# Turning attention weights for former keys in 32x32 squares on VectorE and through device memory, in a two-layer hybrid encoder kernel

## The chip, the core and the metric

The kernel runs on one core of a Trainium2 chip. The metric is the time of one execution in microseconds (us) of device time; lower is better. The kernel before was run three times: 2492.28, 2494.07 and 2495.88 us. The core's engines are TensorE (PE; PEld is its loading of stationary operands), VectorE (DVE), ScalarE (ACT), GpSimd (POOL) and SyncE (SP), which here issues every DMA.

## What is computed

Two layers over a sequence of 2048 frames of width 1024, batch 1. Each layer normalises and modulates its input, maps it by one combined projection, runs two groups of heads on the result, and maps their outputs back by one projection onto the residual. The change touches the second group, four heads of differential attention, shortened here:

```
def diff_branch(q, k, v, z, qn_g, kn_g, lam, lam_init, g_out):
    q = rms_norm(q.reshape(B, S, 4, 2, 64), qn_g) * 64 ** -0.5
    k = rms_norm(k.reshape(B, S, 4, 2, 64), kn_g)
    ...
    s = einsum('bqhmd,bkhmd->bhmqk', qi, k)      # two score maps m per head
    p = softmax(where(key_chunk <= q_chunk, s, -inf), axis=-1)   # chunks of 64 frames
    attn = p[:, :, 0] - lam * p[:, :, 1]
    o = einsum('bhqk,bkhe->bqhe', attn, v)       # v is 128 wide
    return rms_norm(o, g_out) * (1 - lam_init) * silu(z)
```

The other group is a gated linear attention with a recurrent state per chunk. All arrays are float32.

## The kernel before

**Units.** The sequence is cut into four units of 512 frames, u = 0 to 3, and each layer goes through them in order. A unit has dense work (nine items of 512 columns: four attention heads, two groups for the convolved inputs, the gate, two halves of the output projection), the gated linear part, and the four attention heads. In the dense work every operand is split into a high and a low part, so one product is three matmuls of 128x512; an item is 8 contraction steps x 4 banks x 3 matmuls. The program calls the banks `acc`, the split weights `w`, and the split input `hhi` and `hlo`. The weights are split once per layer, kept in device memory (`wd`), and loaded again by each later unit as tiles of 512 KB, one per contraction step; pool `p_w` holds four.

**Attention.** `attn_gen(l, u, hd)` does one head of one unit. Keys and values of former units lie in device memory (`KD`, `VD`) and are loaded as `Kj` and `Vj`; those of the unit itself are `Kt` and `Vt`. The head's 512 queries are taken in four row blocks of 128, qt = 0 to 3. `scores(qt, m)` multiplies queries by keys into PSUM (`sc`); VectorE moves the negated scores to a row `s` of 128 x 2048 in SBUF with a running minimum, and ScalarE takes the exponent of the row. When both maps of a row block are there, VectorE combines them in place into the attention weights `at`, by `scalar_tensor_tensor` over pieces of 512 (`s<-s,r` in the profile); the second row, `b`, is free then.

`pv(qt)` multiplies the weights by the values. That product contracts over keys, so keys must lie along the partitions, while a row of `at` has queries there. Each 128x128 square is turned by a transpose on TensorE against the identity (`tp<-ident,s`); ScalarE copies four squares at a time from PSUM to an SBUF tile (`aT<-tp`), and each square is the stationary operand of one float32 matmul with 128 columns of values (`po<-Vj,aT`, `po<-Vt,aT`), which the profile shows as two weight loads and two matmuls. Row block qt of unit u has 4u + qt + 1 squares, 4u of them for former units: 1088 squares in the whole kernel.

**Pools.** `p_s` has four score rows, so the scores of two row blocks are ahead; `p_at` holds three tiles of turned weights. `p_q` has five slots of 4 KB per partition, used by the input blocks `xt`, by three tiles of the gated linear part, and by the split queries `qh` and `ql` of each head. `ps_t` holds four PSUM banks, shared by `sc`, `tp` and `po`.

**Order of the work.** The code is written as streams (dense, attention, query/key, gated linear, preparation), merged by the TensorE time that each step declares. `record` only stores each operation. Then `Program.order`, a list scheduler that knows the pools, a cost for each operation (`cost`) and delays between engines (`LAT`), and models the DMA queue as one server, sets the order on each engine; `best_order` repeats that with small changes and keeps the best by its own reckoning. What comes out is a fixed order for each engine: on the chip each engine runs its own list in order, and waits where an operand is late. SP's list is one too: a DMA that has to wait holds up all DMAs listed behind it. Since all operations are issued at one place, line 370, the profile is read by tile names rather than lines.

Of the kernel before, what the change touches and what calls it, by code (L numbers as in the profile page):

```python
# [12 lines left out]
F32 = mybir.dt.float32  # L13
# [9 lines left out]
P = 128  # L23
D = 1024
KT = D // P
UT = 512
# [94 lines left out]
class Program:  # L121
# [53 lines left out]
    @staticmethod  # L175
    def cost(e, method, args, kw, out):
        n = math.prod(out.shape[1:])
        if e == "S":
            return math.prod(out.shape) * 4 / 360.0
        if e == "T":  # L180
            if method == "transpose":
                return 110
            rate = {F32R: 2.4, BF16: 2.4, F32: 0.6}[args[2].dt]
            if rate == 0.6 and args[1].shape[1] < P:
                return 54 if args[1].shape[0] == CH else 60
            return max(n * 0.444, 112 * args[1].shape[1] / P) if rate == 2.4 else max(n / rate, 216) + 6
# [187 lines left out]
def trunk_kernel(ctx, tc, x, c, w_ada, b_ada, norm_g, w_in, conv_w, w_gk, b_gk, gla_norm_g,  # L374
# [232 lines left out]
    def done(*ev):  # L607
        events[ev] = clock[0]
# [224 lines left out]
    def gla_gen(l, u):  # L833
# [146 lines left out]
        for hd in range(4):  # L980
# [3 lines left out]

    KD = [[dram.tile([P, 2, UT], F32, name=f"kd{u}_{h}") for h in range(4)] for u in range(NU - 1)]
    VD = [[dram.tile([P, TT, P], F32, name=f"vd{u}_{h}") for h in range(4)] for u in range(NU - 1)]
    WD = [[[dram.tile([P, 2, 512], F32, name=f"wd{l}_{i}_{k}") for k in range(KT)] for i in range(9)]
          for l in range(L)]
    XD = [dram.tile([UT, D], F32, name=f"xd{u}") for u in range(NU)]
# [27 lines left out]
    def qk_gen(l, u, hd):  # L1017
        y = layers[l]
        key = l * NU + u
        yield need("hev", key, hd, lag=6.0)  # L1020
        qk, Vt, sz = HD.pop((key, hd))
        qh = p_q.tile([P, 2, UT], F32R, tag="q", name="qh")
        ql = p_q.tile([P, 2, UT], F32R, tag="q", name="ql")
        Kt = p_kv.tile([P, 2, UT], F32R, tag="K", name="Kt")
        for g in range(2):
            ps = tp()
            for t in range(TT):
                T.transpose(ps[:, t * P:(t + 1) * P], qk[t][:, g * P:(g + 1) * P], ident)
# [16 lines left out]
        done("qkT", key, hd)  # L1045

    def attn_gen(l, u, hd):
# [12 lines left out]
        Ks.append(Kt)  # L1060
# [3 lines left out]
        def scores(qt, m):  # L1064
# [23 lines left out]
            if m == 1:  # L1088
# [9 lines left out]
                q_t[qt] = (at, r, clock[0] + 0.6 + 0.00083 * nk + 0.4 + 0.5 + 0.8)  # L1098

        def pv(qt):  # L1100
            at, r, t0 = q_t.pop(qt)
            nk = u * UT + (qt + 1) * P
            qs = slice(qt * P, qt * P + P)
            nb = nk // P
            o_ = po()[:, 0:P]
            if t0 > clock[0]:
                yield pe(0, t0 - clock[0])
            prev = None

            def mmv(g0, w, aT):  # L1110
                for i in range(w):
                    T.matmul(o_, aT[:, i * P:(i + 1) * P], Vs[g0 // 4][:, i, :],
                             start=(g0 + i == 0), stop=(g0 + i == nb - 1))

            for g0 in range(0, nb, 4):
                w = min(4, nb - g0)
# [3 lines left out]
                aT = p_at.tile([P, 512], F32, tag="aT", name="aT")  # L1120
                A.copy(aT[:, 0:w * P], ps[:, 0:w * P])
                yield pe(0.11 * w, 0 if prev else 0.9)
                if prev:
                    mmv(*prev)
                    yield pe(0.22 * prev[1], 0.2)
                prev = (g0, w, aT)
            if nb > 4:
                yield pe(0, 0.7)
            mmv(*prev)
            yield pe(0.22 * prev[1])  # L1130
# [6 lines left out]
            V.scalar_tensor_tensor(sz[:, qt, :], o_, wq, sz[:, qt, :], op0=ALU.mult, op1=ALU.mult)  # L1137

        seq = [(qt, m) for qt in range(TT) for m in range(2)]
        order = [("s", 0), ("s", 1), ("s", 2), ("s", 3)]  # L1140
        for qt in range(TT):
            order.append(("c", qt))
            for x_ in (2 * qt + 4, 2 * qt + 5):
                if x_ < 2 * TT:
                    order.append(("s", x_))
        for k_, i in order:
# [196 lines left out]
```

## Time and profile before

| | |
|---|---|
| median of 3 runs | 2494.07 us |
| lowest and highest | 2492.28, 2495.88 us |
| span of the profiled execution | 2491.1 us, clock 0.999 |
| TensorE busy | 2454.7 us |
| VectorE busy | 1690.3 us |
| ScalarE busy | 1369.9 us |
| moved by DMA | 473.99 MB, 190 GB/s in the mean |

For the profiled execution the page gives its span alone, 2491.1 us, from the first to the last instruction; no time of its own stands beside that. The median of the three timed runs is 3.0 us above the span. Busy time of TensorE is no measure of its spare time, because matmuls overlap in the pipeline and their ends are modelled. More is told by the chain of work that ended last, in which each step is followed back to what released it: there, a stretch that belongs to TensorE alone is one that gets shorter when TensorE has less to do. First layer: unit 1 is worked on from about 300 us, unit 2 from about 600, unit 3 from about 900 to 1130. Second layer: units 1, 2 and 3 from about 1560, 1870 and 2180 us; the last instruction is at 2491.

### The profile page before, as it was taken

The numbers are of one execution on the slowest core, as the hardware profiler recorded it, in microseconds if no ns is written. First come the engines' busy times: TensorE is split into PE (matmuls) and PEld (weight loads), VectorE is DVE, ScalarE is ACT, GpSimd is POOL, SyncE is SP. The second block draws the span as 40 slices with busy tenths as digits, with TensorE's granted clock in tenths as the row PEclk, the third lists the DMA queues.
The fourth block names the chain that finished last, engine by engine and source line by source line (L and its number), as shares of the span: only waits on it lengthen the run. The fifth ranks groups of instructions, "written<-read, shape, count | busy, mean of one in ns | idle before, by whom it ended". The sixth has DMA issues, their size and how long they took to land.

```text
span 2491.1 us, 40404 instructions
## 1 busy us (share of the span) xinstructions
PE 2454.7 (99%) x13923; PEld 2027.2 (81%) x13923; DVE 1690.3 (68%) x4993; ACT 1369.9 (55%) x3080; POOL 133.0 (5%) x424
## 2 busy tenths in 40 slices
PE   8999999999999999999999999999999999999998
PEld 5787788888888878888788777888788888888887
DVE  4879777772768727678764894667636777276873
ACT  5757545572556724556763583556625567155652
POOL 0001000000000000000000010000000000000000
PEclk9999999999999999999999999999999999999999
DMA  8778866457453563435367877455464444633343
GB/s 264 265 238 294 309 236 213 149 193 240 146 175 117 195 211 121 157 127 173 112 206 258 283 254 266 164 179 180 165 227 157 150 155 155 217 132 127 124 148 127
DMA packets 204684, 473.99 MB, mean 190 GB/s; under 512 B 20736, under 2 KB 82368, under 8 KB 204480
## 3 DMA queue, kind: packets, MB, share of 16 engines
q1 hardware_dynamic: 204480, 471.41, 55.6%
q8 instruction: 111, 1.82, 0.3%
q14 instruction: 93, 0.76, 0.1%
HBM read 360.19 MB, written 111.15 MB: 189 GB/s over the span
## 4 chain that ended last, share of the span: by engine, by line
PE 83%; DVE 8%; DMA 4%; ACT 2%; issue 2%; POOL 0%; SPq 0%; POOLq 0%; DVEq 0%; ACTq 0%
PE acc L370 54%; PE sc L370 11%; PE po L370 10%; PE tp L370 8%; DVE s L370 3%; DMA wr<-in_w_ada_dram 2%; DVE t L370 1%; DMA wd<-w 1%; DVE am L370 1%; DVE w L370 1%; DMA xt<-in_x_dram 1%; ACT s L370 1%; DMA raw<-in_w_in_dram 0%; ACT qh L370 0%; SPq L370 0%
## 5 line engine op out<-in xcount | busy, mean ns | idle before, releaser
L370 PE MATMUL acc<-w,hhi 128*128 128x512 f32 x2560 | 832.5, 402 | 0.6 <-DVE rt L370 0.3
L370 PEld LDWEIGHTS acc<-w,hhi 128*128 128x128 f32 x2560 | 463.1, 189 | 85.1 <-issue 3.0
L370 PE MATMUL acc<-w,hlo 128*128 128x512 f32 x1280 | 505.6, 395 | 0.0
L370 ACT ACTIVATE s<-s,mx 128x512 f32<-128x512 f32 (+15 forms) x256 | 308.2, 1204 | 238.1 <-DVE s L370 236.5
L370 PE MATMUL acc<-hhi,w 128*128 128x512 f32 x1024 | 363.4, 401 | 0.0
L370 PE MATMUL acc<-w,oh 128*128 128x512 f32 x1024 | 332.4, 397 | 1.0 <-ACT oh L370 0.8
L370 DVE TENSOR_SCALAR_CACHE_REDUCE s<-sc,mx 64x64 f32<-64x64 f32 (+5 forms) x640 | 308.6, 485 | 36.2 <-PE sc L370 15.2
L370 PEld LDWEIGHTS acc<-w,hlo 128*128 128x128 f32 x1280 | 240.8, 188 | 49.4 <-DVE hlo L370 0.4
L370 PEld LDWEIGHTS acc<-w,oh 128*128 128x128 f32 x1024 | 189.5, 188 | 41.5 <-DVE t L370 2.1
L370 PEld LDWEIGHTS acc<-hhi,w 128*128 128x128 f32 x1024 | 191.7, 188 | 35.8 <-DVE z L370 0.3
L370 DVE TENSOR_SCALAR_CACHE_REDUCE s<-sc 128x512 f32<-128x512 f32 (+4 forms) x256 | 158.3, 622 | 75.4 <-PE sc L370 72.0
L370 PE MATMUL po<-Vj,aT 128*128 128x128 f32 x1536 | 204.2, 276 | 2.5 <-ACT aT L370 2.2
L370 PE MATMUL acc<-w,ol 128*128 128x512 f32 x512 | 202.8, 397 | 0.0
L370 PE MATMUL acc<-hlo,w 128*128 128x512 f32 x512 | 201.0, 393 | 0.0
L370 PEld LDWEIGHTS po<-Vj,aT 128*128 128x128 f32 x1536 | 190.8, 192 | 11.4 <-ACT aT L370 5.8
L370 DVE SCALAR_TENSOR_TENSOR s<-s,r 128x512 f32<-128x512 f32 (+2 forms) x320 | 197.8, 667 | 2.7
L370 ACT COPY aT<-tp 128x512 f32<-128x512 f32 (+2 forms) x320 | 163.3, 521 | 61.3 <-PE tp L370 59.6
L370 ACT COPY rw<-acc 128x256 f32<-128x256 f32 x128 | 48.0, 375 | 252.7 <-PE acc L370 252.4
L370 PE MATMUL tp<-ident,s 128*128 128x128 f32 x1088 | 174.3, 275 | 6.9 <-DVE s L370 6.2
L370 PEld LDWEIGHTS tp<-ident,s 128*128 128x128 f32 x1088 | 132.8, 141 | 42.5 <-issue 8.9
L370 PE MATMUL sc<-Kj,qh 128*128 128x512 f32 x384 | 158.5, 413 | 1.6 <-DVE s L370 0.9
L370 ACT CAST w<-raw 128x512 fp32r<-128x512 f32 x152 | 93.5, 627 | 107.4 <-PE acc L370 89.5
(184 smaller groups left out, 3708.5 us busy)
## 6 DMA issues: line engine op xcount, KB each, us to landing
w<-wd SPq DMA_DIRECT2D x424, 512.0 KB, 4.1
wd<-w SPq DMA_DIRECT2D x144, 512.0 KB, 4.5
raw<-in_w_in_dram SPq DMA_DIRECT2D x120, 256.0 KB, 4.7
Kj<-kd SPq DMA_DIRECT2D x48, 512.0 KB, 4.6
wr<-in_w_ada_dram SPq DMA_DIRECT2D x128, 128.0 KB, 3.7
kd<-Kt SPq DMA_DIRECT2D x24, 512.0 KB, 2.6
Vj<-vd SPq DMA_DIRECT2D x48, 256.0 KB, 3.8
wr<-in_w_ada_dram SPq DMA_DIRECT2D x8, 1024.0 KB, 9.6
```

The costliest lines, as they stand in the source:

```text
L370: getattr(self.engines[e], method)(*[real(a) for a in args], **{k: real(v) for k, v in kw.items()})
```

## The change

For former units, in units 1 and 2 with all four heads and in unit 3 with heads 0 to 2 (`turned`), the squares are no longer turned on TensorE. After the combination, VectorE turns the former part of the row in 32x32 squares, from `at` into `b`, in two instructions that each take every other group of 128 columns and write every other element. One DMA writes `b` to device memory (`AD`) in pieces of 1 KB; another reads it back into `at` with the 32-row groups put in place, in pieces of 64 elements (256 bytes). The keys then lie on the partitions in an order of their own, so the values of former units are kept a second time in that order (`VP`, copied from `VD` within device memory once per head and unit) and read from there. `pv` takes the stationary operands straight from `at`, every second element. The squares of the unit itself (1 to 4 per row block) are still turned on TensorE, first of all, and copied by ScalarE into `b`. Where nothing is turned (unit 0; head 3 of unit 3) the old path remains, with `b` in place of the tile `aT`.

`p_s` grows to five rows, `p_at` is gone, `p_q` shrinks to four slots. Turned heads begin with five score rows instead of four. The planner reckons DMAs whose last dimension is 64 at 256 bytes per ns instead of 360, and the stream waits 7 us of TensorE time longer before `pv`.

```diff
-            return math.prod(out.shape) * 4 / 360.0
+            return math.prod(out.shape) * 4 / (256.0 if out.shape[-1] == 64 else 360.0)
...
-    p_s = pool("p_s", 4)
-    p_at = pool("p_at", 3)
+    p_s = pool("p_s", 5)
...
-    p_q = pool("p_q", 5)
+    p_q = pool("p_q", 4)
...
+            SY.dma_start(VP[u][hd].rearrange("(j b) t e -> j b (t e)", b=4),
+                         VD[u][hd].rearrange("(b j) t e -> j b (t e)", b=4))
...
+        turned = u > 0 and (u < NU - 1 or hd < 3)
...
-            SY.dma_start(b, VD[j][hd])
+            SY.dma_start(b, (VP if turned else VD)[j][hd])
...
+                if turned:
+                    turn_blocks(at, b, AD[u][TT * (hd % 2) + qt])
...
+        def turn_blocks(at, b, dr):
+
+            n = u * UT
+            src = at[:, 0:n].rearrange("p (g k a i) -> p g k a i", k=2, a=4, i=32)
+            dst = b[:, 0:n].rearrange("p (g a i k) -> p g k a i", a=4, k=2, i=32)
+            for k in range(2):
+                V.transpose(dst[:, :, k], src[:, :, k])
+            SY.dma_start(dr.rearrange("g p b n -> p g (b n)"), b[:, 0:n].rearrange("p (g n) -> p g n", n=256))
+            SY.dma_start(at[:, 0:n].rearrange("p (h n) -> p h n", n=64),
+                         dr.rearrange("g (a j) b n -> (j b) (g a) n", a=4))
...
+            if turned:
+                pairs = at[:, 0:u * UT].rearrange("p (g m k) -> p g k m", k=2, m=P)
+                flip(4 * u, qt + 1)
+                yield pe(0.11 * (qt + 1), 0.9)
+                mmv(4 * u, qt + 1, flat, True, False)
+                yield pe(0.22 * (qt + 1), AFTER)
+                for j in range(u):
+                    mmv(4 * j, 4, lambda k: pairs[:, k // 2, k % 2, :], False, j == u - 1)
+                    yield pe(0.88)
...
-        order = [("s", 0), ("s", 1), ("s", 2), ("s", 3)]
+        ahead = 5 if turned else 4
+        order = [("s", x_) for x_ in range(ahead)]
```

How the order changes is seen best in unit 3 of the second layer. On TensorE, before, around the last row block of head 0 (`tp<-ident,s` turns squares of weights, `po` multiplies by values, `acc` is dense work, `tp<-ident,rw` turns queries and keys of a later head):

```order
L370 MATMUL tp<-ident,s 128x128 x4
L370 MATMUL po<-Vj,aT 128x128 x4
L370 MATMUL acc<-w,hhi 128x512 x2
L370 MATMUL acc<-w,hlo 128x512
L370 MATMUL tp<-ident,rw 128x128 x4
L370 MATMUL tp<-ident,s 128x128 x4
L370 MATMUL po<-Vj,aT 128x128 x4
L370 MATMUL acc<-w,hhi 128x512 x2
L370 MATMUL acc<-w,hlo 128x512
```

On the same engine and at the same place, in the changed kernel:

```order
L370 MATMUL tp<-ident,s 128x128 x4
L370 MATMUL acc<-w,hhi 128x512 x2
L370 MATMUL acc<-w,hlo 128x512
L370 MATMUL acc<-w,hhi 128x512 x2
L370 MATMUL acc<-w,hlo 128x512
L370 MATMUL po<-Vt,s 128x128 x4
L370 MATMUL tp<-ident,z 128x128 x2
L370 MATMUL po<-Vj,s 128x128 x12
```

The transposes of former keys are gone. Only the unit's own four squares are turned, and the twelve products with former values stand in one run.

On SP, before, in the same unit, the weight tiles (`w<-wd`) of items 2 and 5, then those of item 3 and the next head's keys:

```order
L370 DMA w<-wd_5_4_14997 128x1024
L370 DMA w<-wd_5_5_15003 128x1024
L370 DMA w<-wd_5_6_15017 128x1024
L370 DMA w<-wd_5_7_15027 128x1024
L370 DMA w<-wd_3_0_15308 128x1024
L370 DMA w<-wd_3_1_15325 128x1024
L370 DMA Kj<-kd_2_2307 128x1024
```

On SP in the changed kernel, at the same place (`ad<-s` writes a turned row block, `s<-ad` reads it back):

```order
L370 DMA w<-wd_5_4_14550 128x1024
L370 DMA w<-wd_5_5_14556 128x1024
L370 DMA ad_5_11289<-s 128x6x256
L370 DMA s<-ad_5_11289 128x24x64
L370 DMA w<-wd_5_6_14570 128x1024
L370 DMA w<-wd_5_7_14580 128x1024
L370 DMA Kj<-kd_2_2308 128x1024
L370 DMA Kj<-kd_2_5130 128x1024
L370 DMA ad_6_11471<-s 128x6x256
```

A write and its reading back now stand between the weight loads, here without anything between the two, so that the loads behind them are issued only when the write has landed. Of the 88 pairs in the list, 12 stand like this and the other 76 have one to five other DMAs between write and read.

More of the change, by code (lines that the diff above doesn't have):

```diff
@@ L986, in trunk_kernel @@
     VD = [[dram.tile([P, TT, P], F32, name=f"vd{u}_{h}") for h in range(4)] for u in range(NU - 1)]
+    VP = [[dram.tile([P, TT, P], F32, name=f"vp{u}_{h}") for h in range(4)] for u in range(NU - 1)]
+    AD = [[dram.tile([2 * u, P, 4, 64], F32, name=f"ad{u}_{t}") for t in range(2 * TT)] if u else None
+          for u in range(NU)]
     WD = [[[dram.tile([P, 2, 512], F32, name=f"wd{l}_{i}_{k}") for k in range(KT)] for i in range(9)]
@@ L1043, in qk_gen @@
             SY.dma_start(VD[u][hd], Vt)
+            SY.dma_start(VP[u][hd].rearrange("(j b) t e -> j b (t e)", b=4),
+                         VD[u][hd].rearrange("(b j) t e -> j b (t e)", b=4))
         HD[key, hd, "q"] = (qh, ql, Kt, Vt, sz)
         done("qkT", key, hd)
+    WAIT, AFTER = 7.0, 0.0
     def attn_gen(l, u, hd):
@@ L1097, in scores @@
                                            op0=ALU.mult, op1=ALU.add)
-                q_t[qt] = (at, r, clock[0] + 0.6 + 0.00083 * nk + 0.4 + 0.5 + 0.8)
+                if turned:
+                    turn_blocks(at, b, AD[u][TT * (hd % 2) + qt])
+                q_t[qt] = (at, b, r, clock[0] + 0.6 + 0.00083 * nk + 0.4 + 0.5 + 0.8 + (WAIT if turned else 0))
+        def turn_blocks(at, b, dr):
[7 more added lines that the diff above has]
+                         dr.rearrange("g (a j) b n -> (j b) (g a) n", a=4))
         def pv(qt):
-            at, r, t0 = q_t.pop(qt)
-            nk = u * UT + (qt + 1) * P
+            at, b, r, t0 = q_t.pop(qt)
             qs = slice(qt * P, qt * P + P)
-            nb = nk // P
+            nb = 4 * u + qt + 1
             o_ = po()[:, 0:P]
@@ L1107, in pv, with flip @@
                 yield pe(0, t0 - clock[0])
[L1108 to L1116, printed above, removed]
+            def flip(g0, w):
                 ps = tp()
@@ L1119, in pv, with mmv @@
                     T.transpose(ps[:, i * P:(i + 1) * P], at[:, (g0 + i) * P:(g0 + i + 1) * P], ident)
[L1120 to L1130, printed above, removed]
+                A.copy(b[:, g0 * P:(g0 + w) * P], ps[:, 0:w * P])
+            def mmv(g0, w, aT, first, last):
+                for i in range(w):
+                    T.matmul(o_, aT(g0 + i), Vs[(g0 + i) // 4][:, (g0 + i) % 4, :],
+                             start=first and i == 0, stop=last and i == w - 1)
+            flat = lambda k: b[:, k * P:(k + 1) * P]
+            if turned:
[7 more added lines that the diff above has]
+                    yield pe(0.88)
+            else:
+                prev = None
+                for g0 in range(0, nb, 4):
+                    w = min(4, nb - g0)
+                    flip(g0, w)
+                    yield pe(0.11 * w, 0 if prev else 0.9)
+                    if prev:
+                        mmv(*prev, flat, prev[0] == 0, False)
+                        yield pe(0.22 * prev[1], 0.2)
+                    prev = (g0, w)
+                if nb > 4:
+                    yield pe(0, 0.7)
+                mmv(*prev, flat, prev[0] == 0, True)
+                yield pe(0.22 * prev[1])
             junk = p_t.tile([P, P], F32, tag="th", name="junk", bufs=2)
@@ L1139, in attn_gen @@
         seq = [(qt, m) for qt in range(TT) for m in range(2)]
-        order = [("s", 0), ("s", 1), ("s", 2), ("s", 3)]
+        ahead = 5 if turned else 4
+        order = [("s", x_) for x_ in range(ahead)]
         for qt in range(TT):
             order.append(("c", qt))
-            for x_ in (2 * qt + 4, 2 * qt + 5):
+            for x_ in (2 * qt + ahead, 2 * qt + ahead + 1):
                 if x_ < 2 * TT:
```

## The prediction

> **What bounds the kernel now.** I read the page first: its span, the busy times, the chain of work that ended last, and the DMA queue.
>
> ```profile
> span 2491.1 us, 40404 instructions
> PE 2454.7 (99%) x13923; PEld 2027.2 (81%) x13923; DVE 1690.3 (68%) x4993; ACT 1369.9 (55%) x3080; POOL 133.0 (5%) x424
> PE 83%; DVE 8%; DMA 4%; ACT 2%; issue 2%; POOL 0%; SPq 0%; POOLq 0%; DVEq 0%; ACTq 0%
> q1 hardware_dynamic: 204480, 471.41, 55.6%
> ```
>
> TensorE carries 83% of the chain, VectorE is busy two thirds of the time, the DMA engines a little over half. That is a mean over stages, so the chain comes next by stretches: one in the first layer's unit 1, one where unit 3 of that layer ends, and one in the second layer's unit 1.
>
> ```profile
> by line: PE acc L370 43.3%; DMA wr<-in_w_ada_dram 12.8%; DMA wd<-w 9.4%; DVE t L370 7.4%; DVE s L370 7.4%; DVE am L370 5.8%; issue 4.1%; PE tp L370 2.8%; ACT t L370 2.0%; PE sc L370 1.9%; PE po L370 1.8%; ACT ub L370 1.1%; POOL wq L370 1.1%
> by line: PE acc L370 28.3%; DVE s L370 14.5%; PE po L370 13.9%; PE sc L370 11.8%; PE tp L370 8.4%; DMA raw<-in_w_in_dram 7.7%; issue 4.4%; ACT s L370 2.1%; DVE ol L370 2.1%; DVE hlo L370 1.4%; DVE nb L370 1.2%; DVE xt L370 0.7%; POOL wq L37
> by line: PE acc L370 66.9%; PE sc L370 12.1%; PE po L370 11.8%; PE tp L370 9.4%
> ```
>
> The last of them is TensorE alone: whatever TensorE no longer does there comes off the end. In the first, DMAs and VectorE set the pace for a good third of the time. The busy times by stretch say how full the other engines are (busy us and count for PE, PEld, DVE, ACT, POOL, then the granted clock, the DMA share and GB/s):
>
> ```profile
> core 0: us, PE busy (x) PEld busy (x) DVE busy (x) ACT busy (x) POOL busy (x), PEclk, DMA share, GB/s
> 1300.00:1560.00 260.00, 257.36 (x1337) 207.10 (x1337) 173.74 (x476) 136.46 (x329) 14.35 (x40) 1.00 0.77 264
> 1800.00:1870.00 70.00, 70.00 (x325) 57.89 (x324) 25.49 (x77) 17.99 (x40) 0.16 (x2) 1.00 0.67 232
> 1870.00:2110.00 240.00, 239.84 (x1474) 202.94 (x1473) 175.86 (x528) 145.64 (x325) 15.94 (x51) 1.00 0.44 153
> 2180.00:2400.00 220.00, 219.92 (x1362) 188.17 (x1361) 165.63 (x489) 124.69 (x250) 9.26 (x34) 1.00 0.38 130
> ```
>
> Units 2 and 3 of the second layer lie mostly in the last two rows. VectorE has 64 of 240 us free there and 54 of 220, and the DMA engines are idle more than half of the time.
>
> **What TensorE saves.** A turned row block of unit u drops 4u transposes. Row blocks per layer: 16 in unit 1, 16 in unit 2, 12 in unit 3; so 16 x 4 + 16 x 8 + 12 x 12 = 336 squares, 672 in both layers, of the 1088. Their price is read from the chain inside unit 3 of the first layer, as is that of the products that stay (start, us, what):
>
> ```profile
> 1014.86 0.87 PE tp L370 x8
> 1049.61 1.78 PE po L370 x16
> 1612.61 12.27 PE acc L370 x54
> ```
>
> A transpose is 0.87 / 8 = 0.109 us (the group of these transposes has a mean duration of 275 ns, which is pipelined and not the price). 672 x 0.109 = 73.2 us off TensorE. The 64 squares of the first layer's unit 1, 7.0 us, lie where other things set the pace, and I count them at nothing: 66.2 us are left on the path. The order on TensorE keeps the balance: the dense work done when each head ends is about what it was, so the saving isn't made up of work that is merely left for the tail.
>
> ScalarE loses 168 copies of four squares. It isn't on the path, so its row brings nothing but room:
>
> ```profile
> L370 ACT COPY aT<-tp 128x512 f32<-128x512 f32 x224 | 129.3, 584 | 45.5 <-PE tp L370 44.3
> L370 DVE TENSOR_TENSOR rw<-rw,rq 128x256 f32<-128x256 f32 x128 | 45.8, 419 | 0.8
> L370 DVE TENSOR_TENSOR w<-raw,w 128x512 fp32r<-128x512 f32 x152 | 103.8, 687 | 56.9 <-ACT w L370 55.8
> L370 DVE TENSOR_SCALAR xt<-xt,xrs 128x1024 f32<-128x1024 f32 x32 | 24.0, 750 | 5.4 <-POOL xrs L370 5.0
> ```
>
> **What VectorE gains.** No transpose of VectorE is in the trace. The nearest rows are its float32 passes over SBUF: 419 ns for 256 columns, 687 ns for 512, hence about 955 ns for 768 by the same step. Two instructions per row block: 32 x 0.419 + 32 x 0.687 + 24 x 0.955 = 58.3 us per layer, 117 us in all. The bound below is the rate of the last row, 0.73 ns per column: 63 us. The bound above is a pass at half speed, because each writes every other element: 234 us. I take 117. In 2180 to 2400 it makes 165.6 + 22.9 = 188.5 us of VectorE in 220 - 15.7 = 204.3 us, 92%; in 1870 to 2110 it makes 197.9 of 226, 88%. It still fits, but VectorE runs its list in order: behind a transpose stand the moves of scores out of PSUM, and behind those TensorE's next scores. I count a tenth of what units 2 and 3 save (544 squares, 59 us): 6 us lost.
>
> **What the DMA queue gains.** Each way 86,016 columns x 128 partitions x 4 bytes = 44.0 MB: 43,008 pieces of 1 KB out, 172,032 of 256 bytes back. The price of a piece comes from the queue's rows in two stretches, one of many small pieces (0 to 125 us), one of mostly large ones (2200 to 2300 us): packets, MB, share of the 16 engines.
>
> ```profile
> q1 hardware_dynamic: 28536, 32.98, 81.2%
> q1 hardware_dynamic: 3744, 12.85, 36.8%
> ```
>
> In engine time these are 1624 us and 589 us; solved for a fixed price and a price by size: 0.0060 us per packet plus 44.1 us per MB. So 0.0173 us for 256 bytes and 0.051 us for 1 KB. Reading back: 172,032 x 0.0173 / 16 = 186 us of all engines; writing 137; the second copy of the values, 24 x 128 packets of 2 KB, 18. Together 341 us: the share goes from 55.6% to about 69%. For a row block of unit 3 it is 3.3 us back and 2.5 out. In 2180 to 2400, 0.38 x 220 + 12 x 5.8 = 153 us of 204: 0.75; in 1870 to 2110, (0.44 x 240 + 16 x 3.8) / 226 = 0.74. Today 0.67 (1800 to 1870) goes with a full TensorE, and at 0.77 (1300 to 1560) little is lost. Hence no lack of rate, but waits in the queue. Landing times and SP's own waits:
>
> ```profile
> w<-wd SPq DMA_DIRECT2D x424, 512.0 KB, 4.1
> wd<-w SPq DMA_DIRECT2D x144, 512.0 KB, 4.5
> SPq L370 <- PE acc L370: 1087.4, 348, 12.1
> 505.43 7.62 DMA xt<-in_x_dram
> ```
>
> A pair of weight tiles feeds 24 matmuls, which take 24 x 12.27 / 54 = 5.5 us in a purely dense stretch and about 9 us where scores lie between; a load lands after 4.1 us, so it has 1.4 to 5 us to spare. A read of 3.3 us ahead of it, or SP standing at a read whose write takes 4.5 us to land, can use that up. On SP the weight loads are what stands behind, and today SP waits mostly for TensorE to free a tile, so a load is issued with nothing in hand. Bounds: nothing, if the loads always find their room, and 341 us, if every added microsecond stood in front of a needed load. I take 0.15 us for each of the 88 row blocks, 13 us, because the spare time covers most of it. The 24 copies of values wait on SP in the same way for a write of 256 KB, with weight loads behind them; they are far fewer and are counted in the 13. The row block's own way (about 2 us on VectorE, 4.5 us out, some 5 us back) is hidden by the scores of the fifth row and by dense work; without that cover it would cost 12 us each time.
>
> **The pools.** The rows of `p_s` and the old path of untouched heads keep all instructions and cost nothing, since `b` isn't needed before its row block ends; if it were, a score row would come late by a product's 2 us. With four slots in `p_q` instead of five, an input block or the next head's queries can wait for a slot. The chain has one such wait, the 7.6 us for `xt` in the last row above. Between 0 and seven units of 7.6 us, 53; I take 3, because the queries of a head are free as soon as its last scores are done.
>
> **Stationary operands with a gap.** The products with former values now read every second element. A product costs 1.78 / 16 = 0.111 us per load and matmul, set by the load. No row shows a load with a gap. Bounds: nothing and twice the time, 1344 x 0.111 = 149 us; nor can it be a gain, as the load still brings 128 columns. I take nothing, since the nearest row is the same load without the gap, with the same 128 columns of four bytes. The Trainium skill, SBUF — State Buffer, section "Door 1: The DMA port swizzle", gives SBUF lines of 16 bytes and asks for at least two hits per line at full rate; a step of 8 bytes gives just two, so by that page nothing is the right end, and no run here shows it yet.
>
> **The sum.** 73.2 - 7.0 - 6 - 13 - 3 = 44 us, so the span goes from 2491.1 to 2447. The median lies 3.0 us above the span: 2494.1 - 44 = **2450 us**. If waits came out at half or half as much again (11 us either way) and unit 1 gave its 7 us after all, 2432 to 2461.
>
> **The rivals.**
>
> *Late weights.* The queue, not TensorE, sets the pace in units 2 and 3. For it: the pairs without anything between them on SP, and a share of 0.75 where it was 0.38. Against it: 0.67 with no loss. It decides from 0.5 us more per row block: 88 x 0.5 = 44. At 0.5 to 0.6 us the time is 2494 to 2503, at a quarter of that 2461. My middle for it is 2495. The Trainium skill, DMA: Bandwidth & Descriptors, section Specifications, speaks against this change: line rate needs transfers of at least 512 bytes, and below that the engine reads, modifies and writes. If that doubled the price of a 256-byte piece, reading back would take 372 us, the share would be 0.94 in 2180 to 2400, and this rival would hold; no run here shows it yet.
>
> *VectorE full.* With the upper price, 234 us, 2180 to 2400 would hold 211 us of VectorE in 204, and 1870 to 2110 220 in 226. Unit 3 would save nothing, unit 2 half of its 14 us: 7 + 2 x 7 = 21 us less some waits, about 2478.
>
> *Slow loads, the slower side.* If loads with a gap take half as long again or twice as long, 75 to 149 us come on top: 2525 to 2599. It decides from 44 / 1344 = 0.033 us per load, a third more than today's 0.111.
>
> **How the numbers follow.** Chances: forecast 0.60, late weights 0.18, VectorE full 0.11, slow loads 0.11. Runs of this kernel spread by 0.14%, so 0.2% (5 us) is about what can be told from no change. Faster: 0.60 + 0.10 of VectorE full + 0.06 of late weights = 0.76. Same: 0.06 of late weights and 0.01 of VectorE full, 0.07. Slower: slow loads with 0.11 and 0.06 of late weights, 0.17. The range starts at the whole saving, 2494 - 73 = 2421, and reaches into late weights, to 2503; slow loads and a little of late weights are left out. The likeliest case's own range is 2432 to 2461.
>
> **What would show it.** Right: 416 transposes `tp<-ident,s`, the chain in 1600 to 1700 still all TensorE, a transposed pass on VectorE below 1 us for 768 columns, reading back about 3 us of queue, products at 0.111 us. Late weights would show as waits of weight loads for `w<-wd` in units 2 and 3; VectorE full as score products that wait for `s`; slow loads as `po<-Vj` far above 0.111 us in the chain. Wrong altogether: a time above 2503, or a saving much over 73 us.

## The result, and the profile after

The changed kernel takes 2474.88 us in the median of four runs (2474.00 to 2476.23); the kernel before, run beside it, 2493.18 (2491.25 to 2495.88). The ratio is 0.993, 95% interval 0.9916 to 0.9944. It is faster, and the time lies in the range of the prediction, but the gain is 18 us where the sum had 44.

The page after, with the same lines as before:

```profile
span 2472.4 us, 39660 instructions
...
PE 2408.5 (97%) x13251; PEld 1962.4 (79%) x13251; DVE 1778.4 (72%) x5169; ACT 1289.0 (52%) x2912; POOL 138.2 (6%) x424
...
q1 hardware_dynamic: 425792, 565.79, 70.7%
...
PE 43%; DMA 4%; DVE 4%; ACT 1%; issue 1%; SPq 0%; POOL 0%; POOLq 0%; DVEq 0%; ACTq 0%
```

TensorE has 672 matmul instructions fewer (13923 to 13251) and is busy for 46.2 us less. Its idle time, span less busy, was 2491.1 - 2454.7 = 36.4 us and is 63.9 now. 46.2 - 27.5 = 18.7 us, just the difference of the spans: TensorE was relieved, and gave more than half of that back as waiting. A wait can also cost more than itself. The trace has five stretches of 3.4 us in which the granted clock is 0.50, 17 us in all, where the one before had one of 6.8 us; in the 3.4 us ahead of each of the five, TensorE was busy for 1.8 us or less. At half clock 17 us lose at most 8.5 us, against 3.4 before. (The shares of the chain add up to 53% only: here it could be followed back no further than about 1100 us, so they are not set against those of before.) By stretches, the same ones as before:

```profile
1300.00:1560.00 260.00, 258.16 (x1342) 208.12 (x1341) 174.86 (x478) 136.90 (x329) 14.86 (x40) 1.00 0.77 268
1800.00:1870.00 70.00, 70.00 (x328) 58.15 (x327) 33.87 (x98) 21.64 (x49) 0.29 (x2) 1.00 0.66 224
1870.00:2110.00 240.00, 238.30 (x1385) 195.89 (x1384) 188.30 (x549) 134.39 (x293) 16.42 (x50) 1.00 0.74 235
2180.00:2400.00 220.00, 213.48 (x1257) 178.18 (x1256) 185.72 (x522) 108.69 (x220) 10.62 (x36) 0.99 0.73 212
```

In 2180 to 2400 TensorE had 0.08 us idle before and has 6.52 now; in 1870 to 2110, 0.16 and 1.70. The DMA share rose from 0.44 and 0.38 to 0.74 and 0.73, as forecast (0.74, 0.75). What TensorE waits for (us in all, times, longest), the largest of those that hang on the new way or grew. Rows with PEld are idle time before weight loads, rows with PE idle time before matmuls. Both often show one and the same stretch (the longest wait for the read-back, 5.0 us of the loads and 4.8 us of the matmuls, ends at 1006.44 us in both), so the two rows of a product must not be added, and TensorE's idle time is that of the matmuls.

```profile
PEld po L370 <- DMA s<-ad: 17.8, 19, 5.0
...
PEld tp L370 <- DVE z L370: 16.0, 24, 4.5
...
PEld sc L370 <- DVE s L370: 13.1, 42, 1.0
...
PE po L370 <- DMA s<-ad: 11.4, 10, 4.8
...
PE tp L370 <- DVE z L370: 8.1, 8, 4.0
...
PEld acc L370 <- DMA w<-wd: 7.0, 10, 2.4
...
PE acc L370 <- DMA w<-wd: 3.5, 4, 2.0
```

Products now wait for the read-back: weight loads 19 times, for 17.8 us, and in 10 of these cases the matmuls stand idle too, for 11.4 us, up to 5 us at a time. Before, the rows of the weight loads for scores, for `z` and for the dense work, and one of SP's, read:

```profile
PEld sc L370 <- DVE s L370: 8.1, 21, 1.0
...
PEld tp L370 <- DVE z L370: 4.4, 7, 1.8
...
PEld acc L370 <- DMA w<-wd: 1.2, 3, 0.4
```

```profile
SPq L370 <- DVE s L370: 19.0, 19, 1.7
```

And the new instructions themselves, the squares on VectorE by shape (count, busy us, mean ns, idle us before), the two transfers of a unit-3 row block (KB, median us from issue to landing), and what SP waits for between its DMAs:

```profile
L370 DVE STREAM_TRANSPOSE s<-s 128x768 f32<-128x768 f32 x48 | 46.6, 972 | 0.1
...
L370 DVE STREAM_TRANSPOSE s<-s 128x512 f32<-128x512 f32 x64 | 44.9, 704 | 0.1
...
L370 DVE STREAM_TRANSPOSE s<-s 128x256 f32<-128x256 f32 x64 | 27.5, 436 | 0.1
```

```profile
ad<-s SPq DMA_DIRECT2D x24, 768.0 KB, 4.7
s<-ad SPq DMA_DIRECT2D x24, 768.0 KB, 5.9
```

```profile
SPq L370 <- PE acc L370: 687.5, 322, 11.4
SPq L370 <- DVE s L370: 258.9, 99, 9.0
...
SPq L370 <- DMA ad<-s: 130.2, 51, 7.5
```

The squares came out at their price, 119 us against 117. SP stands for 259 us until something in a row `s` is done on VectorE; in the trace 223 of them are at 70 of the 88 writes, whose squares are not ready. For 130 us it stands at 51 of the 88 read-backs, whose write hasn't landed. Weight loads stand behind both. In exchange, its waits for TensorE's dense work, nearly all ahead of weight loads, fell from 1087 to 687 us, so most of the new standing takes the place of standing that was there before.

### The profile page after: what moved, and what is told of

Same layout as the page of the kernel before. It is cut to its first block, busy times and chain, and to the rows that moved or that the text cites. A ratio compares the mean times of both kernels' runs of the same rounds, so it can differ in the third digit from the quotient of the medians.

```text
span 2472.4 us, 39660 instructions
## 1 busy us (share of the span) xinstructions
PE 2408.5 (97%) x13251; PEld 1962.4 (79%) x13251; DVE 1778.4 (72%) x5169; ACT 1289.0 (52%) x2912; POOL 138.2 (6%) x424
## 3 DMA queue, kind: packets, MB, share of 16 engines
q1 hardware_dynamic: 425792, 565.79, 70.7%
## 4 chain that ended last, share of the span: by engine, by line
PE 43%; DMA 4%; DVE 4%; ACT 1%; issue 1%; SPq 0%; POOL 0%; POOLq 0%; DVEq 0%; ACTq 0%
PE acc L370 29%; PE sc L370 6%; PE po L370 5%; PE tp L370 3%; DVE s L370 2%; DMA ad<-s 2%; DMA s<-ad 1%; DMA w<-wd 1%; SPq L370 0%; DMA wr<-in_w_ada_dram 0%; ACT s L370 0%; DMA xt<-xd 0%; POOL wq L370 0%; DVE w L370 0%; DVE z L370 0%
## 5 line engine op out<-in xcount | busy, mean ns | idle before, releaser
L370 PE MATMUL acc<-hhi,w 128*128 128x512 f32 x1024 | 352.1, 398 | 1.4 <-DVE z L370 1.4
L370 PE MATMUL po<-Vj,s 128*128 128x128 f32 x1536 | 201.7, 283 | 12.7 <-DMA s<-ad 11.4
L370 PEld LDWEIGHTS po<-Vj,s 128*128 128x128 f32 x1536 | 193.4, 197 | 23.9 <-DMA s<-ad 17.8
L370 POOL MEMSET s<- 64x64 f32 x256 | 38.5, 151 | 2058.1 <-PE po L370 1384.7
L370 PE MATMUL sc<-Kj,ql 128*128 128x512 f32 x384 | 153.0, 398 | 0.0
L370 DVE TENSOR_TENSOR w<-raw,w 128x512 fp32r<-128x512 f32 x152 | 103.3, 686 | 61.0 <-ACT w L370 60.1
```

The source lines that it names most:

```text
L370: getattr(self.engines[e], method)(*[real(a) for a in args], **{k: real(v) for k, v in kw.items()})
```

## The experiments

Four theories of where the gain went. *Late trip*: a row block's way over VectorE, out and back is not hidden, and products wait for it. *Crowded queue*: the new traffic makes other transfers late. *Full VectorE*: the squares make scores late. *Poor order*: the new order on TensorE, with four `p_q` slots, is worse whatever the squares and DMAs cost. All times are medians; each ratio is to the kernel before, run beside it, and its interval is about 4 us to each side, so that a difference of two of them is sure to some 5 us.

### One part left out, the order kept

The planner still reckons with every operation, so each engine keeps its order; those in `left_out` are only not issued. Line numbers shift by two to four.

```diff
+            if i in self.left_out:
+                continue
...
             for k in range(2):
                 V.transpose(dst[:, :, k], src[:, :, k])
+                prog.left_out.add(len(prog.ops) - 1)
             SY.dma_start(dr.rearrange("g p b n -> p g (b n)"), b[:, 0:n].rearrange("p (g n) -> p g n", n=256))
+            prog.left_out.add(len(prog.ops) - 1)
             SY.dma_start(at[:, 0:n].rearrange("p (h n) -> p h n", n=64),
                          dr.rearrange("g (a j) b n -> (j b) (g a) n", a=4))
+            prog.left_out.add(len(prog.ops) - 1)
```

*no_turn* has the first of the three added lines in `turn_blocks`, *no_trip* the other two, *neither* all of them.

> The changed kernel in its own fixed order, with the transposes on VectorE and both DMAs of each turned row block left out; the products read the unturned weights. Four theories of where some 45 us of the saving went. Late trip: a product waits until its row block is back from device memory. Full VectorE: the added passes delay the moves of scores. Crowded queue: the added traffic delays weight tiles and keys. Poor order: the list itself, made by the planner, has lost it. The first three expect about 2435 us here (2474.9 less some 40), the poor order expects 2465 to 2475.

> The changed kernel in its own order, with both DMAs of each turned row block left out and the transposes on VectorE kept; the products read the unturned weights. Late trip and crowded queue expect 2435 to 2450 us, full VectorE 2465 to 2470, poor order 2470 to 2475.

> The changed kernel in its own order, with the transposes on VectorE left out and both DMAs kept, so that the second score row makes the trip in place of the turned weights. Full VectorE expects 2440 to 2450 us. Late trip expects 2462 to 2470, because each trip starts about 2 us sooner. Crowded queue and poor order expect 2470 to 2475.

Measured: *neither* 2437.59 us (0.9767, 0.9751 to 0.9783); *no_trip* 2450.89 (0.9828, 0.9813 to 0.9842); *no_turn* 2470.58 (0.9906, 0.9891 to 0.9921). Without squares and transfers 56 us are gained, so the two together eat 37 of them. The transfers are the larger part: 24 us when they are taken away, 33 when they are added to a kernel without squares. The squares cost 13 us alone, and only 4 beside the transfers: it seems that in part they hide behind the same waits. Full VectorE falls as the main cause; 13 us are left to it at most. In the profile of *no_turn* the score products wait for VectorE as little as in the kernel before (7.7 us against 8.1; 13.1 after), while the products' wait for the read-back has grown:

```profile
PEld po L373 <- DMA s<-ad: 23.6, 22, 4.9
...
PE po L373 <- DMA s<-ad: 16.1, 16, 4.7
...
PEld sc L373 <- DVE s L373: 7.7, 24, 0.8
```

### What of the transfers costs: the landing, the traffic, or the small pieces

In these runs, too, the planner reckons with the kernel as it is, so the order is kept; `instead` gives single operations other operands when they are issued. First try: the read-back lands in `b`, and the products read the row unturned, so that they need not wait for it.

```diff
+            args = self.instead.get(i, args)
...
+            prog.instead[len(prog.ops) - 1] = (b[:, 0:n].rearrange("p (h n) -> p h n", n=64),
+                                              prog.ops[-1][2][1])
```

> The changed kernel in its own order with all transposes and all DMAs, but what is read back lands in the second score row and the products read the unturned first one, so that no product waits for a trip while VectorE and the queue have the same work. Late trip expects 2440 to 2455 us. Crowded queue, full VectorE and poor order expect 2470 to 2475.

2489.86 us (0.9989, 0.9978 to 1.0001), 15 us slower than after, which none of the theories expected. It answers another question: `b` is the next score row's buffer, and now it comes free only when the read-back has landed. VectorE, which fills it, waits, and TensorE's scores wait for VectorE:

```profile
DVE s L372 <- DMA s<-ad: 18.2, 7, 4.9
```

```profile
PEld sc L372 <- DVE s L372: 30.7, 43, 4.4
...
PE sc L372 <- DVE s L372: 18.5, 11, 4.0
```

So I let the same pieces land in device memory, in tiles `AE` that nobody reads (`other` below), and nothing waits for them.

```diff
+                    turn_blocks(at, b, AD[u][TT * (hd % 2) + qt], AE[u][TT * (hd % 2) + qt])
...
+            prog.instead[len(prog.ops) - 1] = (other, prog.ops[-1][2][1])
```

> The read-back goes from device memory to another place in device memory in the same pieces, so that no instruction waits for it; the products read the row before it is turned. Squares, order, queue and bytes are those of after. Late trip (what costs is that the products, and the row's next user, wait for the landing): 2449 to 2455, as with the transfers left out. Crowded queue (what costs is that the other transfers, of weights, keys and values, and the score row's release, come later): 2468 to 2476. In between, the two share the 24 us as the time says.

2461.04 us (0.9871, 0.9856 to 0.9885): between the two. 2474.88 - 2461.04 = 14 us are the wait for the row block's way. In the two profiles, whose spans differ by 13.4 us, 8.4 of them are idle time of TensorE (63.9 against 55.5) and 5.0 longer busy time of the same matmuls; up to 3 of these 5 can be the clock, with 17 us at half clock against 10. 2461.04 - 2450.89 = 10 us are the transfers themselves, since *no_trip* differs from this run in them only: their bytes, SP's standing for them, and the row `b`, which stays taken until the write has read it. The waits say whom they hurt; first *no_trip*, then this run:

```profile
PEld tp L373 <- DVE z L373: 9.9, 23, 1.4
...
PEld acc L373 <- DMA w<-wd: 3.6, 5, 1.3
...
PE tp L373 <- DVE z L373: 3.0, 5, 1.0
...
PE acc L373 <- DMA w<-wd: 1.7, 2, 0.9
```

```profile
PEld tp L372 <- DVE z L372: 14.9, 25, 4.6
...
PEld acc L372 <- DMA w<-wd: 10.6, 15, 2.9
...
PE tp L372 <- DVE z L372: 7.1, 6, 4.2
...
PE acc L372 <- DMA w<-wd: 5.8, 9, 2.4
```

In the rows of the matmuls the wait for split weights goes from 1.7 to 5.8 us and that for the gated output `z` from 3.0 to 7.1. The growth of the second is a single wait of 4.2 us, at 1162 us, and no weights are in its chain. A write needed 9.0 us to land and so held its score row; GpSimd, which is the next to write to this row, stood until then, and the factor `wq` that `z` needs is listed behind that. The changed kernel has the same wait, 4.0 us at 1169. Last, the read-back in pieces of 1 KB; the 32-row groups are then not put in place.

```diff
+            prog.instead[len(prog.ops) - 1] = (at[:, 0:n].rearrange("p (g n) -> p g n", n=256),
+                                              dr.rearrange("g p b n -> p g (b n)"))
```

> The second transfer of a row block reads back the same bytes in pieces of 1 KB, in the order in which they were written, so the blocks are not put in place; order, squares, waits and bytes are those of after. Late trip: a read-back of three units takes 768 x 0.051 / 16 = 2.4 us of the queue, not 3.3, so some 0.9 us of each wait goes, 3 to 8 us in all: 2467 to 2472. Crowded queue: the share of the transfers falls by some 5 points (some 100 us of 16 engines' time), and with it most of what the traffic costs: 2455 to 2465. If the 256-byte pieces cost no more than the 1-KB ones: 2475.

2468.67 us (0.9905, 0.9889 to 0.9922), with the queue at

```profile
q1 hardware_dynamic: 296768, 565.79, 67.6%
```

So some 6 us hang on the piece size, with an interval from about 1 to 12; the middle is late trip's figure. In engine time the queue falls from 0.707 x 2472.4 = 1748 us to 0.676 x 2463.9 = 1666: 82 us. With 1 KB at 0.051 us, the prediction's price, a 256-byte piece is therefore estimated at (137 + 82) x 16 / 172,032 = 0.0204 us, not 0.0173.

### The stationary operand with a gap

```diff
-                pairs = at[:, 0:u * UT].rearrange("p (g m k) -> p g k m", k=2, m=P)
+                pairs = at[:, 0:u * UT].rearrange("p (g k m) -> p g k m", k=2, m=P)
```

> The products of weights and values take 128 neighbouring words of the turned row as their stationary operand, not every second one, so the keys of a block are no longer those of its values; order, squares and transfers are those of after. Gapped operand (a weight load that reads every second word is slower, and the product behind it with it): 1344 products x 6 ns = 8 us faster than after, 2465 to 2469. The prediction's bound at nothing: 2475, as after.

2472.48 us (0.9921, 0.9905 to 0.9938), against 0.993 for after: 2 us, which the intervals don't tell from nothing. The products' rows (minimum, median, maximum ns), after and then here:

```profile
L370 PEld LDWEIGHTS po<-Vj,s x1536: 186/196/331, 361.8 to 2437.8; 128*128 128x128 f32 x192
L370 PE MATMUL po<-Vj,s x1536: 270/281/582, 361.8 to 2438.0; 128*128 128x128 f32 x192
```

```profile
L370 PEld LDWEIGHTS po<-Vj,s x1536: 186/192/333, 363.1 to 2434.2; 128*128 128x128 f32 x192
L370 PE MATMUL po<-Vj,s x1536: 270/275/581, 363.1 to 2434.4; 128*128 128x128 f32 x192
```

A load from every second word is 4 ns longer, its matmul 6 ns. 1344 x 6 = 8 us is the most that it can be.

### What TensorE's saving is worth

Here the kernel before keeps its own order, and the 672 transposes and their copies are not issued; the products read the row unturned. `first` is the number of the group's first operation; `unflipped(g0)` is true where the change turns the group otherwise.

```diff
+                    if unflipped(g0):
+                        prog.instead[len(prog.ops) - 1] = (o_, at[:, (g0 + i) * P:(g0 + i + 1) * P],
+                                                           Vs[g0 // 4][:, i, :])
...
                 A.copy(aT[:, 0:w * P], ps[:, 0:w * P])
+                if unflipped(g0):
+                    prog.left_out.update(range(first, len(prog.ops)))
```

> The kernel before in its own order, with the 672 transposes that the change removes from TensorE, and their copies on ScalarE, left out, so that the products read the weights unturned; two slots, rows and dues are as before. Poor order (the 17 us that lay between the 73.2 of the transposes and the 56 of the run with neither squares nor transfers were lost to the new order and its four q slots): 2493 - 73 = 2420, 2416 to 2428. Waits that come out elsewhere (TensorE without the transposes waits more for others, whatever the order): 2432 to 2442, as that run.

2446.38 us (0.9811, 0.9796 to 0.9825): 48 of 73 us, less than either theory expected. Its page:

```profile
span 2445.1 us, 38827 instructions
...
PE 2389.4 (98%) x13251; PEld 1961.4 (80%) x13251; DVE 1688.7 (69%) x4993; ACT 1289.4 (53%) x2912; POOL 133.9 (5%) x424
```

TensorE is busy for 65.3 us less and idle for 55.7 us instead of 36.4. This list, which was set for a longer TensorE, doesn't use the saving whole, even with no new work anywhere; and the new order, with its own slots and rows, does better by 9 us (*neither*), so it is not poor as such. The slot by itself:

```diff
-    p_q = pool("p_q", 5)
+    p_q = pool("p_q", 4)
```

> The kernel before with four slots for q rows, not five, and nothing else; nothing is left out. The prediction's term: 3 us slower, 2494 to 2499. Poor order by the slot: 8 to 15 us slower, 2501 to 2508. No cost: 2493.

2497.13 us (1.0016, 1.0006 to 1.0025): 3 us, as the sum had it. Then the order was reckoned anew for a kernel without squares, transfers and due time:

```diff
-    WAIT, AFTER = 7.0, 0.0
+    WAIT, AFTER = 0.0, 0.0
...
-                if turned:
-                    turn_blocks(at, b, AD[u][TT * (hd % 2) + qt])
```

> After without squares, transfers and due time, in an order that is reckoned for just that; the products read the row unturned. An order fitted to less work can use all of TensorE's 73 us: 2493 - 73 = 2420, with the q slot's 3 and the gapped operand's 2 to 8 up to 2431. TensorE waits for others in any order: 2432 to 2446, as in the two runs without that work.

2428.65 us (0.9747, 0.9731 to 0.9763), 64.5 us under the kernel before, with four slots and the gap in it.

```profile
span 2424.7 us, 38964 instructions
...
PE 2389.1 (99%) x13251; PEld 1962.9 (81%) x13251; DVE 1683.4 (69%) x4993; ACT 1287.9 (53%) x2912; POOL 141.7 (6%) x424
```

TensorE's idle time is 35.6 us, that of before. So the kernel can have the saving, in an order that leaves no room for other things. The 9 us to *neither* are what lies between this order and the one that reckons with the squares, the trip and the due time; which of the three costs them wasn't tried. The second copy of the values stays in all these runs, so what it costs is inside the 64.5 us.

### Other orders of the same work

Four runs in which nothing is left out. *four_rows*:

```diff
-    p_s = pool("p_s", 5)
+    p_s = pool("p_s", 4)
...
-    p_q = pool("p_q", 4)
+    p_q = pool("p_q", 5)
...
-        ahead = 5 if turned else 4
+        ahead = 4
```

> After with four score rows and five q slots, as before had them, and four score rows ahead of the first weights; squares and transfers are those of after, nothing is left out. Poor order by the slot: 8 to 15 us faster than after, 2460 to 2467. Late trip (a row is held through its trip, so the fifth is needed): a score row waits 5 to 10 us for a buffer at each head of units 2 and 3, and it is 2485 to 2520.

2481.25 us (0.9947, 0.9932 to 0.9962), 6 us over after: neither theory's number, and the fifth row is worth little more than the slot it takes. So most of the cover that the prediction gave to that row comes from elsewhere.

*later_due_12*, and *due_4* with 4.0 at the same place:

```diff
-    WAIT, AFTER = 7.0, 0.0
+    WAIT, AFTER = 12.0, 0.0
```

> Where the products of a row block are due is put 12 us behind its weights in the order's reckoning, not 7; nothing else is edited, nothing is left out. Late trip (14 us of it by the run whose read-back lands in device memory): with 5 us more of other work ahead of the products, most of that goes: 2460 to 2468. Crowded queue alone: 2472 to 2478. Slots (rows are held for longer and the score rows behind them wait for a buffer): over 2480.

2512.79 us (1.0087, 1.0069 to 1.0105), 38 us slower than after. As a cure for the late trip this fails. The products do wait less for the landing, but other waits grow by more, and the clock joins in: the profiled execution has a granted clock of 0.990 (0.997 after), and TensorE is busy for 12.5 us more with the same 13251 matmuls (2421.0 against 2408.5) besides 24.8 us more of idle time; 48 us of the trace are at half clock, against 17.

```profile
PEld tp L370 <- DVE s L370: 14.2, 22, 3.7
...
PEld acc L370 <- DMA w<-wd: 13.5, 18, 1.8
...
PEld po L370 <- DMA s<-ad: 13.2, 12, 2.4
...
PE po L370 <- DMA s<-ad: 9.4, 8, 2.1
```

The transposes of the units' own squares wait for the row on VectorE, dense work for its weights (5.6 and 7.0 us after, in the same rows). The time is the one that the theory of the slots gave; which held buffer is to blame was not tried apart. With 14.0 in the same place (*later_due*) there is no time at all, since the list scheduler finds no order: it comes to a point at which no operation that is left has both its operands and its buffers. That, too, speaks for the slots.

> Where the products of a row block are due is put 4 us behind its weights, not 7; nothing else is edited, nothing is left out. Late trip (the products stand too early for the landing): 3 us for a part of 88 row blocks more, 2480 to 2500. Slots (rows are held for too long at 7 as at 12): 2455 to 2470. The due time hardly matters on this side: 2470 to 2480.

2487.03 us (0.9978, 0.9969 to 0.9988), 12 us slower than after. Products that are due earlier wait for the landing longer, the loads 23.5 us against 17.8 and the matmuls 13.4 against 11.4:

```profile
PEld po L370 <- DMA s<-ad: 23.5, 32, 4.4
...
PE po L370 <- DMA s<-ad: 13.4, 18, 4.2
```

That is a part of the 12 us and no more: 10.2 of the 14.9 us between the two spans are longer busy time of TensorE (2418.7 against 2408.5), at a clock of 0.995 against 0.997, and this was not followed further. So 7 us is the best of the three. *units_1_2*:

```diff
-        turned = u > 0 and (u < NU - 1 or hd < 3)
+        turned = 0 < u < NU - 1
```

> Rows of units 1 and 2 alone are turned in the new way; those of unit 3 go through TensorE as before; nothing is left out. 384 of the 672 transposes stay removed. Unit 3 gives nothing (its squares and transfers, the longest ones, cost what its 288 transposes saved): 2465 to 2478. Gain spread as the transposes are (288 of 672 of 18 us lost): 2479 to 2486. TensorE's full price for them: 2475 + 31 = 2506.

2476.97 us (0.9934, 0.9920 to 0.9949): the same as after, with 288 transposes more on TensorE. Turning unit 3 gains nothing that can be told. No run with all its work in it was faster than the changed kernel.

## Why the prediction was right in direction and wrong in size

With these runs the way from 2493 to 2475 can be walked in steps of one thing each (the squares and the transfers share some waits, so in another sequence of steps their two parts would differ). The last three steps lie within one and the same order of the work; the first two compare orders that were reckoned apart, and each difference is sure to some 5 us:

| step | forecast | measured | from |
|---|---|---|---|
| TensorE's saving, unit 1 of layer 1 and the slot taken off | 63 | 64.5 | before, planned_without |
| an order that must leave room for the new work | 0 | -8.9 | planned_without, neither |
| squares on VectorE | -6 | -13.3 | neither, no_trip |
| the transfers and what they hold up | -13 | -10.1 | no_trip, lands_in_memory |
| the row block's own way | 0 | -13.8 | lands_in_memory, after |
| sum | 44 | 18.4 | |

**Right.** The price of a transpose, 0.109 us, and so the saving, with the slot's 3 us in it; whether unit 1 gave its 7 us stays within the interval. The squares' duration. The DMA share (70.7% against 69). The transfers' cost in sum, and that weight loads are among those that pay; the 4 us by way of a held score row and GpSimd are a path that the prediction doesn't have. The operand's gap: nothing was taken, and at most 8 us of 149 came. By the rule of the Trainium skill, SBUF — State Buffer, section "Door 1: The DMA port swizzle", two accesses to each line of 16 bytes, a step of 8 bytes is free; the rows show 196 ns against 192 for the load, and in time nothing that can be told.

**The step that failed** is the sentence on the row block's way: that it "is hidden by the scores of the fifth row and by dense work; without that cover it would cost 12 us each time". The sum has nothing for it, and it took 14 us, more than half of the 25.6 that are missing. The price was about right in the middle (4.7 us out and 5.9 back for unit 3). But the cover was taken from the order's intention, a due time that is put 7 us later, and not from a row. The way doesn't start late: SP is mostly there ahead of time, and in the trace the write is issued 0.07 us after the squares in the median of the 88 row blocks. It is the way itself that is longer than the cover, in 19 row blocks of 88. From the end of the combination to the first product these took 8 to 16 us, the six of them in unit 3 took 13.6 to 15.9. The longest: combined at 990.85, squares done at 994.48, written from 994.54 to 998.22, read back from 998.61 on, and the products start at 1006.44, after 4.8 us in which TensorE had nothing to do. The chain says it too: 1600 to 1700, which the prediction wanted all on TensorE, and 2200 to 2300, in unit 3.

```profile
by line: PE acc L370 48.9%; PE po L370 8.0%; PE sc L370 7.6%; PE tp L370 6.1%; DVE s L370 6.1%; DMA ad<-s 5.2%; DMA s<-ad 4.6%; ACT s L370 2.4%; issue 1.9%; POOL wq L370 1.1%; ACT rw L370 0.9%; ACT Kt L370 0.9%; ACT Vt L370 0.8%; DVE nb L37
...
by line: PE acc L370 37.6%; PE po L370 16.3%; DMA s<-ad 12.9%; DMA ad<-s 11.7%; PE sc L370 11.1%; DVE s L370 5.5%; PE tp L370 3.2%; SPq L370 1.1%; issue 0.4%; DVE r L370 0.3%; POOLq L370 0.0%
```

In the second row a quarter of the time is the trip's; before, 2200 to 2300 was TensorE's alone:

```profile
by line: PE acc L370 55.1%; PE sc L370 18.0%; PE po L370 16.1%; PE tp L370 11.0%
```

In unit 3 the squares, writes and reads are longest, and by *units_1_2*, in an order reckoned anew, they eat the saving of 144 squares per layer, as far as can be told.

Two terms had the wrong size or were missing. The squares cost twice the 6 us, by *no_trip*: a tenth of the saving was a guess, and no row stood behind it. And the sum had no term for the order: it took the saving as if each engine's list were fitted to the new durations, though the list with the new work and the due time in it is another list (8.9 us), and one that isn't fitted again loses 25 of 73 (*before_no_flip*).

That the time still lies in the whole range is owed to the room that the range keeps for rivals; the likeliest case's own range, 2432 to 2461, misses it.

**The rivals.** *Late weights* asked for 44 us from the transfers ahead of weight loads; all that the transfers hold up came to 10 us. The page of the Trainium skill that spoke for it, DMA: Bandwidth & Descriptors, section Specifications (line rate from 512 bytes on), agrees in direction: 256 bytes in 0.0204 us against 1 KB in 0.051 is 1.6 times the price per byte. The prediction's fixed price per packet alone makes that 1.4 (4 x 0.0173 / 0.051). A doubled price, which gives (0.556 x 2491 + 155 + 372) / 2472 = 77% of the queue, did not occur: it is 70.7%. *VectorE full* falls with the squares' 972 ns for 768 columns and with *no_turn*; its 2478 us are near the measured time by luck, since the squares, which were to make that loss, cost 4 us beside the transfers and 13 alone. *Slow loads* falls with *no_gap*.

What stays open: why the order reckoned with the new work is 9 us worse, beyond that it is; how the 14 us divide between the squares' time, the write and the reading back, since moving these two transfers to another engine's queue was not tried; and how far single orders scatter by chance, which the difference of 12 and 38 us for a due time of 4 and 12 us suggests is not little.

## What to carry to other kernels

When work is moved off the engine that sets the end, price three things: the work, the new waits, and the order; here the saving was right to 2 us in 63, and the squares, the waits and the order took 46 us of it. "Hidden by other work" is a claim about two lengths: name the row that shows how long the moved step takes at its slowest, and count the work that the order really puts in front of the step that needs it. On an engine or queue that runs its list in order, count too what a wait there holds up, and which buffers it keeps. Leaving single parts out while the order stays fixed splits such a loss in a few runs.

## What was not expected of the hardware

A 32x32 transpose of float32 on VectorE that writes every other word costs nearly as much as a plain two-operand pass over the same columns: 436, 704 and 972 ns for 256, 512 and 768, a step of 268 ns per 256 columns, where the passes of the kernel before took 419 ns for 256 and 687 for 512. TensorE's float32 load with a step of 8 bytes is 196 ns instead of 192. Pieces of 256 bytes are estimated at 0.0204 us of a DMA engine, against 0.051 for 1 KB. Every stretch at half clock in the trace of the changed kernel, 3.4 us each, follows 3.4 us in which TensorE was busy for 1.8 us or less.
